# Two contraction tiles of both heads in each first weight piece, and products ordered by operand

## The chip, the cores and the metric

The kernel runs on one core of a Trainium2 chip. The metric is the device time of one execution in microseconds (us). Three runs of the kernel before gave 1209.47, 1212.88 and 1213.17 us; their median is 1212.88 us. A further, profiled execution took 1211.85 us.

## The reference

One decoder layer on a sequence of 1024 tokens with 1024 features, all in float32. RMSNorm, one input projection, 8 dilated attention heads beside 4 gated linear recurrences, an output projection with a residual, then a second RMSNorm and a gated MLP with a causal convolution. The change touches only the projection that makes the queries and keys of the first two attention heads:

```python
u = rms_norm(h, norm1_g[layer])
proj = u @ w_in[layer]
aq, ak, av, hq, hf, hi, hg = jnp.split(proj, IN_SPLITS, axis=-1)
attn = dilated_attention(aq.reshape(...), ak.reshape(...), av.reshape(...))
```

## The kernel before, in words

**Layout.** Features lie on the 128 partitions. The input is 8 contraction tiles `c` of 128 features by 1024 tokens; tokens are worked in two halves `hf` of 512. Each float32 operand is split into a high part and a low remainder, and a product is three TensorE matmuls: high weight by high input, high weight by low input, low weight by high input. The row scale of the RMSNorm (`R1`, and its transposed form `R1T`) is applied when a result leaves PSUM, so the products can start before the norm is known.

**Weight pieces.** `Ring` (L48) walks a plan of 256 KB pieces of 128x512. For each it starts a DMA from SyncE's queue into a raw buffer (L66; 5 raw buffers), makes the high part `whi` (L86, on ScalarE, but on VectorE for the very first piece) and the low part `wlo` (L88, on VectorE for keys in `on_vector`, else on GpSimd). Five pieces may be live; pieces in `aside` use other tiles (`thw`, `tlw`), which attention needs later. `done` gives a piece back and calls `fill`, which starts the next one of the plan.

**The first four pieces.** A head's query and key weights are 128 columns by 8 contraction tiles, 1024 numbers on each partition. The plan starts with head 0 tiles 0-3, head 1 tiles 0-3, head 0 tiles 4-7, head 1 tiles 4-7. Those of head 1 are the ones put aside. Then come four pieces of `V0` and four of `V1_0` for the attention values.

**Input.** `load_x` (L389) starts the DMA of one input tile, `scale_x` makes its high part `uhi` on ScalarE (L396) and its low part `ulo` on VectorE (L397). `square_x` and `sum_x` (L403, L408) build the sum of squares. The order of these and of the first four pieces is pinned on the queues by lines 421-445: x0, piece 0, x1, piece 1, x2, x3, pieces 2 and 3, x4 and on.

**Products.** TensorE runs in program order; the other engines are ordered by the scheduler of the framework, except where pinned. `dense` (L451) makes the products of one head and one half: for each `c` the matmuls of L459 (high, high), L461 (high, low input) and L462 (low weight). In the first half the order is head 0 tile 0, head 0 tile 1, head 1 tile 0, head 1 tile 1, and from tile 2 on head 0 and head 1 in turn (L665-670). `busy` (L378) puts matmuls of ones into an unused bank: eight at the start, and by `between` four after the first product, one after the third and two after the first product of tile 1. These make no result.

**Behind it.** The second half follows (L671). After its tile 2, `rms1(0)` makes R1 of the first half, both results of the first half leave PSUM (`evac`, L548-554) and `ring.fill()` starts the first `V0` pieces; pieces of the first heads are given back at tile 3 and tile 7 of the second half. Then come `V0` products (`tok`, L476-478), the scores of head 0 (`score_steps`, L584-596) and the long attention loop, in which the results of the second half leave PSUM. `tok`'s first two results and the scores share two PSUM banks, tag `s`.

Of the kernel before, what the change touches and what calls it, by code (L numbers as in the profile page):

```python
# [17 lines left out]
P = 128  # L18
SEQ = 1024
DM = 1024  # L20
NCT = DM // P
H2 = 512
# [21 lines left out]
def f32(ap):  # L44
    return ap.bitcast(F32)
# [93 lines left out]
class DownMix:  # L139
# [7 lines left out]
    def load(self, f, i, t):  # L147
        self.order(self.nc.sync.dma_start(t, self.w[2 * self.k + f, :, i * H2 : (i + 1) * H2]))
        return t
# [53 lines left out]
def hybrid_kernel(ctx: ExitStack, tc: tile.TileContext, xT, w_qk, w_tok, w_hg, w_out, w_up,  # L203
                  w_down, vecs, amask, hmask, out):
    nc = tc.nc
    PE, DVE, ACT, POOL = nc.tensor, nc.vector, nc.scalar, nc.gpsimd
# [12 lines left out]
    ones = f32(ones_r)  # L219
# [13 lines left out]
    halves = [slice(0, H2), slice(H2, SEQ)]  # L233


    plan = []
# [5 lines left out]
    def want_tok(key, g):  # L242
        for i in range(4):
            plan.append(((key, i), w_tok[g, i // 2, :, (i % 2) * H2 : (i % 2 + 1) * H2]))
# [14 lines left out]
    def want_hg(kind, h):  # L259
        want((kind, h), w_hg[4 * {"hq": 0, "hf": 1, "hg": 2}[kind] + h])  # L260

    for i in range(2):
        for h in range(2):
            plan.append(((("qk", h), i), w_qk[h, :, i * H2 : (i + 1) * H2]))
    want_tok("V0", 0)
    want_tok("V1_0", 1)
    for h in (2, 3, 4):
# [39 lines left out]
            xs = ("a11", "a12", "s1", "s2", "s3", "s4", "a22") if f == 2 else ("a11", "s1", "s2", "s3", "a12", "s4", "a22")  # L307
            plan += [((x, f), getattr(m, x)) for x in xs]
    ring = Ring(nc, ringp, plan)
    ring.on_vector = [("qk", 0), ("qk", 1), "V0"]  # L310

    def col(j):
        return vec[:, j : j + 1]
# [40 lines left out]
    uhi = up_.tile([P, NCT, SEQ], F32R, name="uhi")  # L354
    ulo = up_.tile([P, NCT, SEQ], F32R, name="ulo")
# [5 lines left out]
    def bank(tag, name):  # L361
        return ps1.tile([P, H2], F32, tag=tag, name=name, bufs=2)
# [7 lines left out]
    def aside(i):  # L370
        return tuple(at.tile([P, H2], F32R, tag=x, name=f"{x}w{i}", bufs=TB) for x in ("th", "tl"))

    ring.aside = {(("qk", 1), i): aside for i in range(2)}
    ring.aside["a12", 1] = None

    warm = bank("mm", "warm")

    def busy(n):  # L378
        for _ in range(n):
            PE.matmul(warm[:, :P], ones, ones, start=True, stop=True)  # L380

    busy(8)

    between = {(("qk", 0), 0, 0): (4, 1), (("qk", 0), 0, 1): (2, 0)}
    pin = tc.keep_in_program_order
    xts = {hf: vtile([P, NCT, H2], F32, f"xt{hf}") for hf in range(2)}

# [22 lines left out]
    def rms1(hf):  # L410
        ss = bank("t", f"ss{hf}")
        PE.matmul(ss, ones, sums[hf], start=True, stop=True)
        st = bank("t", f"sst{hf}")
        for i in range(4):
            PE.matmul(st[:, i : i + 1], sums[hf][:, i * P : (i + 1) * P], ones[:, 0:1], start=True, stop=True)
        rstd(R1[:, halves[hf]], rtile(f"ms{hf}"), rtile(f"rt{hf}"), ss, 1.0 / DM)
        tm = rv.tile([P, 64], F32, name=f"rst{hf}")
        rstd(R1T[:, 4 * hf : 4 * hf + 4], tm[:, 0:4], tm[:, 4:8], st[:, 0:4], 1.0 / DM)
# [32 lines left out]
    def dense(key, hf, evac, last, tag="mm"):  # L451

        t = halves[hf]
        ps = bank(tag, f"p{key}{hf}".translate({ord(x): "_" for x in "(', )"}))
        for c in range(NCT):
            hi, lo = ring.get((key, c // 4))
            s = slice((c % 4) * P, (c % 4 + 1) * P)
            b = between.get((key, hf, c), (0, 0))
            PE.matmul(ps, hi[:, s], uhi[:, c, t], start=(c == 0), stop=False)  # L459
            busy(b[0])  # L460
            PE.matmul(ps, hi[:, s], ulo[:, c, t], start=False, stop=False)  # L461
            PE.matmul(ps, lo[:, s], uhi[:, c, t], start=False, stop=(c == NCT - 1))  # L462
            busy(b[1])
            if last and c % 4 == 3:
                ring.done((key, c // 4))
            yield 0.65
        evac(ps)
# [60 lines left out]
    if True:  # L528
# [7 lines left out]
            kls.append(kl)  # L536
        qk = {}

        def qk_half(h, hf, last, tag="mm"):
            t = halves[hf]  # L540

            def evac(ps):
                if hf == 0:
                    qk[h] = (at.tile([P, SEQ], F32R, tag="qs", name=f"qs{h}", bufs=NQ),
                             at.tile([P, SEQ], F32R, tag="kh", name=f"kh{h}", bufs=NQ), kls[h % NQ])
                qs, kh, kl = qk[h]
                x = at.tile([P, H2], F32, tag="x", name=f"x{h}_{hf}")
                DVE.tensor_mul(x, ps, R1[:, t])  # L548
                ACT.mul(qs[0:64, t], x[0:64], DH ** -0.5)
                ACT.copy(kh[64:128, t], x[64:128])  # L550
                DVE.tensor_copy(kh[0:64, t], x[64:128])
                DVE.scalar_tensor_tensor(qs[64:128, t], x[0:64], DH ** -0.5, f32(qs[0:64, t]),
                                         op0=ALU.mult, op1=ALU.subtract)
                DVE.tensor_sub(kl[0:64, t], x[64:128], f32(kh[64:128, t]))
            return dense(("qk", h), hf, evac, last, tag)

        def qk_block(h):
            return [qk_half(h, 0, False), qk_half(h, 1, True)]
# [103 lines left out]
        lo4, hi4, all8 = range(4), range(4, 8), range(8)  # L662
        v0 = [tok("V0", t, v_evac(0), t == 7, "mm" if t > 1 else "s") for t in all8]

        pairs = [[qk_half(h, hf, hf == 1, "o" if hf else "mm") for h in range(2)] for hf in range(2)]  # L665
        for h in (0, 0, 1, 1):
            next(pairs[0][h])
        for c in range(2, NCT):
            for g in pairs[0]:
                next(g)  # L670
        for c in range(NCT):  # L671
            for g in pairs[1]:
                next(g)
            if c == 2:
                rms1(0)
                for g in pairs[0]:
                    next(g, None)
                ring.fill()
        for c in range(NCT):
            square_x(1, c)  # L680
# [29 lines left out]
        for h in range(NH):  # L710
            fill.add(*beside[h])
            for j in range(4):
                nxt = (h, j + 1) if j < 3 else (h + 1, 0)
                sc = score_steps(*nxt) if nxt[0] < NH else iter(())
                n_sc = 0 if nxt[0] == NH else (2 if nxt[1] < 2 else 4)
                va = value_steps(h, j, Ps)
                n_va = 2 * j + 2
                share = cost[h] / 4 / (n_sc + n_va)
                nPs = None
                k = 0  # L720
                if (h, j) == (NH - 1, 3):
                    fill.run(1.6)
                while True:
                    got = next(sc, None)
                    nPs = got or nPs
                    if got:
                        fill.run(share)
                    more = None
                    if not got or k % 2:
                        if h == 0 and k == 1 and j < 2:  # L730
                            next(pairs[1][j], None)
                        more = next(va, 0)
                        if more is None:
                            fill.run(share)
                    if not got and more == 0:
                        break
                    k += 1
                Ps = nPs
            fill.run()
# [16 lines left out]
    with pool("hg", "right") as hg:  # L756
# [13 lines left out]
        def f_half(h, hf, last):  # L770
            def evac(ps):
                nm = f"{h}_{hf}"
                A, B = ht("A", "A" + nm, 2), ht("B", "B" + nm, 2)
                DVE.tensor_mul(A, ps, R1[:, halves[hf]])
                DVE.tensor_scalar_max(A, A, -40.0)
                sigmoid(A, A)

                DVE.tensor_scalar(B, A, lb[:, 2 * NG + h : 2 * NG + h + 1], lb[:, NG + h : NG + h + 1],
                                  op0=ALU.mult, op1=ALU.add)
                ACT.activation(A, A, AF.Ln, bias=lb[:, h : h + 1], scale=lb[:, NG + h : NG + h + 1])  # L780
                gate[h, hf] = [A, B]
            return dense(("hf", h), hf, evac, last)

        def q_half(h, hf, last):
            def evac(ps):
                nm = f"{h}_{hf}"
                E, F = ht("E", "E" + nm, 2), ht("F", "F" + nm)
                DVE.tensor_mul(E, ps, R1[:, halves[hf]])
                DVE.tensor_scalar_max(F, E, -40.0)
                sigmoid(F, F)  # L790
                DVE.tensor_mul(E, E, F)
                gate[h, hf].append(E)
            return dense(("hq", h), hf, evac, last)
# [177 lines left out]
        for n, (h, hf) in enumerate(((0, 0), (0, 1), (1, 0), (1, 1), (2, 0), (3, 0), (2, 1), (3, 1))):  # L971

            at = 4.5 + 3 * n + 0.5 * (n in (0, 7))
            start = at - 1.1 if n == 7 else place["hq", h, hf]
# [264 lines left out]
    with pool("ps2", "left", space=PSUM) as ps2:  # L1239

        def bank2(name):
            return ps2.tile([P, H2], F32, tag="u", name=name, bufs=8)
# [69 lines left out]
        pairs = [(x, y, k) for x, y in STAGES for k in range(NPAIR)]  # L1312
# [86 lines left out]
        for x, y in STAGES:  # L1399
            last = x == "s4"  # L1400
# [9 lines left out]
            ps = [bank2(f"d{x}_{d}") for d in range(KS)]  # L1410
            for k in range(NPAIR):
                hi, lo = ring.get((("dn", x), k))
                ahi, alo = feed.get((y, k))
                for d in range(KS):
                    s = slice(d * P, (d + 1) * P)
# [102 lines left out]
```

## Time and profile before

| What | Value |
|---|---|
| median of three runs | 1212.88 us |
| the profiled execution | 1211.85 us |
| its span, first to last instruction | 1209.9 us |
| outside the span (difference of the two) | 1.95 us |
| mean granted TensorE clock | 0.996 |
| VectorE busy, share of the span | 79% |
| ScalarE busy, share of the span | 52% |
| GpSimd busy, share of the span | 25% |

A row of the timeline gives the start, the time until the end (of the whole group where it ends in xN with N over 1), engine, line, operation, written and read tiles, and in brackets how long the engine stood idle before and what released it. PE is TensorE, DVE VectorE, ACT ScalarE, POOL GpSimd and SPq the queue of SyncE. Matmuls are pipelined: the ends shown overlap the next starts, so a pace is read from the starts. A row of the windows gives the length of the stretch, then each engine's busy time, the granted TensorE clock (1.00 is full), the DMA share and GB/s.

### The profile page before, as it was taken

To read this page: it belongs to the slowest core of one execution; us is meant where nothing else is said; L and a number is where in the kernel's file an instruction comes from. 1 tells how busy PE (TensorE), PEld (TensorE's weight loads), DVE (VectorE), ACT (ScalarE), POOL (GpSimd) and SP (SyncE) were. 2 spreads that over 40 slices of the span, in tenths; PEclk is the share of its full clock that TensorE was granted. 3 is DMA by queue.
4 is the path that set the end of the run, shared out by engine and by line. 5 is a ranking of instruction groups with operands and counts; after the bars stand their busy time and mean duration, and the time that the engine had idled before them with its cause. 6 is when DMAs were issued, how large, how long until landed. Compare 5 with 4: busy or idle time off the path is not lost.

```text
span 1209.9 us, 17468 instructions
## 1 busy us (share of the span) xinstructions
PE 1193.9 (99%) x6014; PEld 1006.8 (83%) x6014; DVE 951.6 (79%) x1792; ACT 627.2 (52%) x1205; POOL 299.2 (25%) x278
## 2 busy tenths in 40 slices
PE   9999999999999999999999999999999999999996
PEld 7988888888888888888888888888888888888886
DVE  8867776666778776484999889898798878957986
ACT  8566667667656655454643343433434444444553
POOL 1254446545001014413221322312223100000000
PEclk9999999999999999999999999999999999999998
DMA  7021112123111123442023322333223267435532
GB/s 257 25 70 54 53 53 80 61 62 115 53 36 53 53 62 113 124 137 96 35 71 114 109 86 101 122 114 109 83 97 122 96 209 252 150 99 156 171 100 92
DMA packets 71817, 122.39 MB, mean 101 GB/s; under 512 B 7344, under 2 KB 17840, under 8 KB 71728
## 3 DMA queue, kind: packets, MB, share of 16 engines
q1 hardware_dynamic: 60928, 101.80, 26.8%
q10 hardware_dynamic: 10800, 19.47, 4.2%
q8 instruction: 47, 0.77, 0.3%
q14 instruction: 42, 0.34, 0.1%
HBM read 97.65 MB, written 23.59 MB: 100 GB/s over the span
## 4 chain that ended last, share of the span: by engine, by line
PE 93%; issue 2%; DVE 2%; ACT 1%; POOL 0%; DMA 0%; SPq 0%; DVEq 0%; ACTq 0%; POOLq 0%
PE p L1125 10%; PE p L1123 10%; PE p L1124 10%; PE ds L1418 3%; PE ds L1417 3%; PE ds L1416 3%; PE po L1027 2%; PE po L1029 2%; PE po L1028 2%; PE da L1418 2%; PE da L1417 2%; PE da L1416 2%; PE S L584 1%; PE piv L513 1%; PE S L585 1%
## 5 line engine op out<-in xcount | busy, mean ns | idle before, releaser
L88 POOL TENSOR_TENSOR wlo<-raww,whi 128x512 fp32r<-128x512 f32 x141 | 207.5, 1482 | 383.5 <-ACT whi L86 274.1
L86 ACT CAST whi<-raww 128x512 fp32r<-128x512 f32 x276 | 168.3, 618 | 190.6 <-DVE raww L120 64.8
L88 DVE TENSOR_TENSOR wlo<-raww,whi 128x512 fp32r<-128x512 f32 x136 | 97.4, 716 | 22.6 <-ACT whi L86 22.5
L86 ACT CAST whi<-r 128x512 fp32r<-128x512 f32 x70 | 43.6, 622 | 83.6 <-PE ds L1417 51.4
L596 POOL TENSOR_SCALAR P<-P,st 128x512 f32<-128x512 f32 (+2 forms) x96 | 56.3, 596 | 110.8 <-DVE st L593 62.2
L587 DVE CUSTOM_DVE_ANT_0 P<-S,mask 128x512 f32<-128x512 f32 (+2 forms) x96 | 52.1, 553 | 29.9 <-PE S L585 29.0
L592 ACT ACTIVATE P<-P,st 128x128 f32<-128x128 f32 (+3 forms) x64 | 49.7, 776 | 32.9 <-DVE st L587 16.6
L623 DVE TENSOR_TENSOR tl<-T,th 128x512 fp32r<-128x512 f32 (+1 forms) x80 | 50.7, 634 | 16.6 <-ACT th L622 15.6
L88 DVE TENSOR_TENSOR wlo<-r,whi 128x512 fp32r<-128x512 f32 x70 | 47.9, 686 | 20.2 <-ACT whi L86 20.1
L1418 PE MATMUL ds<-fhi,wlo 128*128 128x512 f32 x160 | 62.3, 389 | 0.0
L1417 PE MATMUL ds<-flo,whi 128*128 128x512 f32 x160 | 62.3, 389 | 0.0
L1416 PE MATMUL ds<-fhi,whi 128*128 128x512 f32 x160 | 62.2, 389 | 0.0
L1123 PE MATMUL p<-b1h,whi 128*128 128x512 f32 x160 | 62.2, 389 | 0.0
L1124 PE MATMUL p<-b1l,whi 128*128 128x512 f32 x160 | 62.2, 389 | 0.0
L1125 PE MATMUL p<-b1h,wlo 128*128 128x512 f32 x160 | 62.2, 389 | 0.0
L1145 DVE SCALAR_TENSOR_TENSOR cv<-g,vec,cv 128x511 f32<-128x511 f32 (+2 forms) x92 | 56.1, 615 | 4.7 <-ACT cv L1142 3.7
L1390 POOL TENSOR_TENSOR facc<-facc,sqf 128x256 f32<-128x256 f32 x4 | 2.9, 732 | 223.1 <-ACT sqf L1389 223.1
L1152 ACT ACTIVATE cv<-cv 128x512 f32<-128x512 f32 x44 | 27.8, 633 | 55.6 <-DVE cv L1145 55.5
L622 ACT CAST th<-T 128x512 fp32r<-128x512 f32 (+1 forms) x80 | 42.9, 536 | 23.5 <-PE T L615 20.9
L86 ACT CAST fhi<-rawf 128x512 fp32r<-128x512 f32 x70 | 43.1, 616 | 15.2 <-DMA rawf<-spT 6.5
L88 DVE TENSOR_TENSOR flo<-rawf,fhi 128x512 fp32r<-128x512 f32 x70 | 47.9, 684 | 4.0 <-ACT fhi L86 4.0
L1416 PE MATMUL da<-fhi,whi 128*128 128x512 f32 x120 | 46.7, 389 | 0.0
(670 smaller groups left out, 3833.5 us busy)
## 6 DMA issues: line engine op xcount, KB each, us to landing
raww<-in_w_up_dram SPq DMA_DIRECT2D x88, 256.0 KB, 3.1
raww<-in_w_tok_dram SPq DMA_DIRECT2D x52, 256.0 KB, 2.6
rawf<-spT SPq DMA_DIRECT2D x40, 256.0 KB, 2.7
r<-in_w_down_dram SPq DMA_DIRECT2D x40, 256.0 KB, 3.4
raww<-in_w_hg_dram SPq DMA_DIRECT2D x32, 256.0 KB, 2.6
raww<-in_w_out_dram SPq DMA_DIRECT2D x32, 256.0 KB, 2.6
spB<-a ACTq DMA_DIRECT2D x30, 256.0 KB, 2.3
spT<-t ACTq DMA_DIRECT2D x30, 256.0 KB, 2.0
```

What stands on the lines that cost most here:

```text
L86: self.pin(self.high(hi[:, :w], raw))
L88: self.pin(low.tensor_sub(lo[:, :w], raw, f32(hi[:, :w])))
L587: DVE.tensor_tensor_reduce(Pt[:, k0 : k0 + w], S[:, :w], mask[:, m : m + w], -1.0, BIG * 3, op0=ALU.add, op1=ALU.min, accum_out=st[:, k0 / ...
L596: POOL.tensor_scalar(e, e, st[:, 3:4], 1.0, op0=ALU.mult, op1=ALU.mult)
L623: DVE.tensor_sub(tl[:, :n], T[:, :n], f32(th[:, :n]))
L1123: PE.matmul(ps, hi[:, s], bhi, start=(start and n == 0), stop=False)
L1124: PE.matmul(ps, hi[:, s], blo, start=False, stop=False)
L1125: PE.matmul(ps, lo[:, s], bhi, start=False, stop=(stop and n == len(rhs) - 1))
L1145: DVE.scalar_tensor_tensor(dst, x, col(V_CW + j * NFF + f), dst, op0=ALU.mult, op1=ALU.add)
L1416: PE.matmul(ps[d], hi[:, s], ahi, start=(k == 0), stop=False)
L1417: PE.matmul(ps[d], hi[:, s], alo, start=False, stop=False)
L1418: PE.matmul(ps[d], lo[:, s], ahi, start=False, stop=(k == NPAIR - 1))
```

## The change

The four first pieces keep their size and count, but piece `i` now holds tiles 2i and 2i+1 of head 0 and of head 1, side by side. It is read with one DMA of two runs of 256 numbers (1 KB) per partition where before one run of 512 (2 KB) was read. Pieces 1 and 3 are the ones put aside. `first_two` takes the place of the two interleaved `dense` generators: for each tile it issues head 0 and head 1 with (high, high), then both with (high, low input), then both with (low weight, high input). The matmuls of ones between products go into a bank of tag `s`: two after the first pair, and one after each of the next three pairs, so five instead of seven. In the second half each piece is given back after its own pair of tiles, at tiles 1, 3, 5 and 7.

```diff
-    for i in range(2):
-        for h in range(2):
-            plan.append(((("qk", h), i), w_qk[h, :, i * H2 : (i + 1) * H2]))
+    def first_pair(i):
+        def load(ring):
+            t = ring.raw()
+            w = w_qk[0:2, :, 256 * i : 256 * (i + 1)]
+            ring.order(nc.sync.dma_start(t.rearrange("p (h n) -> p h n", h=2), w.rearrange("h p n -> p h n")))
+            return t
+        return load
+    for i in range(4):
+        plan.append((("qk01", i), first_pair(i)))
...
-    ring.on_vector = [("qk", 0), ("qk", 1), "V0"]
+    ring.on_vector = ["qk01", "V0"]
...
-    ring.aside = {(("qk", 1), i): aside for i in range(2)}
+    ring.aside = {("qk01", i): aside for i in (1, 3)}
...
-    between = {(("qk", 0), 0, 0): (4, 1), (("qk", 0), 0, 1): (2, 0)}
...
+        def first_two(hf, tag):
+            t = halves[hf]
+            ps = [bank(tag, f"p01_{hf}_{h}") for h in range(2)]
+            idle = bank("s", "idle") if hf == 0 else None
+            waits = {(0, 0): 2, (0, 1): 1, (0, 2): 1, (1, 0): 1} if hf == 0 else {}
+            for c in range(NCT):
+                hi, lo = ring.get(("qk01", c // 2))
+                for i, (w, u) in enumerate(((hi, uhi), (hi, ulo), (lo, uhi))):
+                    for h in range(2):
+                        s = slice(256 * h + (c % 2) * P, 256 * h + (c % 2 + 1) * P)
+                        PE.matmul(ps[h], w[:, s], u[:, c, t], start=(c == 0 and i == 0), stop=(c == NCT - 1 and i == 2))
+                    for _ in range(waits.get((c, i), 0)):
+                        PE.matmul(idle[:, :P], ones, ones, start=True, stop=True)
+                if hf and c % 2:
+                    ring.done(("qk01", c // 2))
+                yield
+            for h in range(2):
+                qk_evac(h, hf)(ps[h])
+                yield
...
-        pairs = [[qk_half(h, hf, hf == 1, "o" if hf else "mm") for h in range(2)] for hf in range(2)]
-        for h in (0, 0, 1, 1):
-            next(pairs[0][h])
-        for c in range(2, NCT):
-            for g in pairs[0]:
-                next(g)
+        pairs = [first_two(hf, "o" if hf else "mm") for hf in range(2)]
         for c in range(NCT):
-            for g in pairs[1]:
-                next(g)
+            next(pairs[0])
+        for c in range(NCT):
+            next(pairs[1])
             if c == 2:
                 rms1(0)
-                for g in pairs[0]:
-                    next(g, None)
+                for _ in pairs[0]:
+                    pass
                 ring.fill()
```

More of the change, by code (lines that the diff above doesn't have):

```diff
@@ L371, in aside @@
         return tuple(at.tile([P, H2], F32R, tag=x, name=f"{x}w{i}", bufs=TB) for x in ("th", "tl"))
-    ring.aside = {(("qk", 1), i): aside for i in range(2)}
+    ring.aside = {("qk01", i): aside for i in (1, 3)}
     ring.aside["a12", 1] = None
     warm = bank("mm", "warm")
[L378 to L382, printed above, removed]
-    between = {(("qk", 0), 0, 0): (4, 1), (("qk", 0), 0, 1): (2, 0)}
+    for _ in range(8):
+        PE.matmul(warm[:, :P], ones, ones, start=True, stop=True)
     pin = tc.keep_in_program_order
@@ L457, in dense @@
             s = slice((c % 4) * P, (c % 4 + 1) * P)
-            b = between.get((key, hf, c), (0, 0))
             PE.matmul(ps, hi[:, s], uhi[:, c, t], start=(c == 0), stop=False)
-            busy(b[0])
             PE.matmul(ps, hi[:, s], ulo[:, c, t], start=False, stop=False)
             PE.matmul(ps, lo[:, s], uhi[:, c, t], start=False, stop=(c == NCT - 1))
-            busy(b[1])
             if last and c % 4 == 3:
@@ L537, in hybrid_kernel, with qk_evac @@
         qk = {}
+        def first_two(hf, tag):
[17 more added lines that the diff above has]
+                yield
         def qk_half(h, hf, last, tag="mm"):
+            return dense(("qk", h), hf, qk_evac(h, hf), last, tag)
+        def qk_evac(h, hf):
             t = halves[hf]
@@ L554, in evac @@
                 DVE.tensor_sub(kl[0:64, t], x[64:128], f32(kh[64:128, t]))
-            return dense(("qk", h), hf, evac, last, tag)
+            return evac
         def qk_block(h):
@@ L730, in hybrid_kernel @@
                         if h == 0 and k == 1 and j < 2:
-                            next(pairs[1][j], None)
+                            next(pairs[1])
                         more = next(va, 0)
```

## The prediction

> **What bounds the kernel now.** I read the page first, for its span and the busy time of the engines.
>
> ```profile
> span 1209.9 us, 17468 instructions
> PE 1193.9 (99%) x6014; PEld 1006.8 (83%) x6014; DVE 951.6 (79%) x1792; ACT 627.2 (52%) x1205; POOL 299.2 (25%) x278
> ```
>
> TensorE is busy for 1193.9 of 1209.9 us, so at most 16 us of the span are without a matmul. Then I asked the waits of TensorE over the whole span; its columns are microseconds in total, times, and the longest.
>
> ```profile
> PE T L612 <- POOL P L596: 2.6, 1, 2.6
> PE warm L380 <- DVE ones L229: 1.1, 1, 1.1
> PE p__qk___0_0_211 L459 <- DVE whi L86: 0.8, 1, 0.8
> PE S L584 <- DVE st L587: 0.8, 2, 0.4
> PE p L1125 <- POOL wlo L88: 0.5, 1, 0.5
> PE ssf L1365 <- POOL facc L1390: 0.3, 1, 0.3
> ```
>
> The waits sum to 6.1 us. Only 0.8 us of them lie where the change works, at the first real product, and they end with the first weight piece's high part. The largest, 2.6 us, lies some 50 us behind it. The windows show what that one costs:
>
> ```profile
> 58.00:61.00 3.00, 1.95 (x12) 1.43 (x10) 2.97 (x7) 1.51 (x4) 1.95 (x2) 1.00 0.00 0
> 61.00:64.00 3.00, 1.34 (x8) 1.24 (x9) 1.58 (x7) 2.31 (x6) 2.08 (x3) 0.90 0.24 87
> 64.00:67.00 3.00, 3.00 (x14) 2.71 (x13) 1.76 (x5) 1.07 (x2) 1.86 (x4) 0.53 0.25 87
> ```
>
> In the third stretch TensorE is busy throughout, but at a granted clock of 0.53. Lost clock is 0.10 x 3 + 0.47 x 3 = 1.7 us. So this stall is worth 2.6 + 1.7 = 4.3 us, far more than anything in the start. It will carry two rivals.
>
> The timeline of the first microseconds shows the place of the change.
>
> ```profile
> 4.38 1.13 DVE L86 CAST whi<-raww 128x512 fp32r<-128x512 f32 x1 [3.25 <-DMA raww<-in_w_qk_dram]
> 5.66 0.47 PE L459 MATMUL p__qk___0_0_211<-uhi,whi 128*128 128x512 f32 x1 [0.83 <-DVE whi L86]
> 5.97 1.05 PE L380 MATMUL warm<-ones 128*128 128x128 f32 x8
> 6.16 1.53 DVE L397 SCALAR_TENSOR_TENSOR ulo<-xt,vec,uhi 128x512 fp32r<-128x512 f32 x2
> 6.18 0.72 ACT L396 ACTIVATE uhi<-xt,vec 128x512 fp32r<-128x512 f32 x1 [1.65 <-DMA xt<-in_xT_dram]
> 6.96 0.50 PE L461 MATMUL p__qk___0_0_211<-ulo,whi 128*128 128x512 f32 x1
> 7.53 0.38 PE L380 MATMUL warm<-ones 128*128 128x128 f32 x2
> 7.98 0.61 PE L380 MATMUL warm<-ones 128*128 128x128 f32 x4
> 8.24 0.69 DVE L88 TENSOR_TENSOR tlw<-raww,thw 128x512 fp32r<-128x512 f32 x1 [0.55 <-ACT thw L86]
> 8.90 0.39 PE L459 MATMUL p__qk___1_0_225<-uhi,thw 128*128 128x512 f32 x1
> 10.29 0.39 PE L459 MATMUL p__qk___0_0_211<-uhi,whi 128*128 128x512 f32 x1
> ```
>
> The last row is head 0's first product of tile 2. From 8.90 to 10.29 lie the six products of head 1's first two tiles, so one product takes 1.39 / 6 = 0.23 us. A filler matmul of ones leaves two records: eight records in 1.05 us make four fillers of 0.26 us. From 6.96 to 10.29 TensorE issues eleven products and three fillers (the six records at 7.53 and 7.98): 11 x 0.23 + 3 x 0.26 = 3.31 of 3.33 us. So from 6.96 us on TensorE never waits in the kernel before. The second weight piece, split at 8.24 + 0.69 = 8.93 us, does not hold it up, though the order by heads looks as if it would. The only slack that the change can use lies ahead of 6.96 us, and the end of that is set by the low part of the first input tile, not by weights: two VectorE operations run 6.16 to 7.69, so the first is done at about 6.92.
>
> **The change part by part.**
>
> *The products.* Before 6.96 us the kernel before issues one product (head 0) and four fillers. The changed one issues two products and two fillers: 5.66 + 2 x 0.23 + 2 x 0.26 = 6.64 us, then it waits 0.3 us for that low part. The two dropped fillers therefore bring nothing; they covered a wait. From 6.96 us on the changed kernel needs ten products and three fillers to reach tile 2: 10 x 0.23 + 3 x 0.26 = 3.08, so 10.04 where the old one takes 3.31 by the same prices. The gain is one product, 0.23 us. Everything else that `first_two` does is the same number of products in another order.
>
> *The pieces.* Each row of a piece is now read as two runs of 1 KB. No such load stands in the busy start of the trace. The nearest rows are the later value pieces, which have just this shape (line 252), against loads with runs of 2 KB (line 66 between 30 and 120 us). First stands the landing of line 252, then that of line 66; then the queue's row for the stretch of 30 to 120 us (2 KB) and for 200 to 250 us (mostly 1 KB).
>
> ```profile
> DMA to landing us min/median/max: 2.4/2.6/3.3
> DMA to landing us min/median/max: 2.3/2.6/3.0
> q1 hardware_dynamic: 2433, 4.43, 15.6%
> q1 hardware_dynamic: 4481, 4.56, 29.9%
> ```
>
> The medians say that 1 KB runs cost nothing; the least differ by +0.1 and the greatest by +0.3. Below nothing I go as far as the least differ, to -0.1. The queue's rows say otherwise: 0.156 x 16 engines x 90 us / 2433 = 92 ns for a packet of mostly 2 KB, and 0.299 x 16 x 50 / 4481 = 53 ns for one of mostly 1 KB. A piece is 8 packets of 2 KB per engine, 0.74 us, or 16 of 1 KB, 0.85 us. I take 0.11 us, since the start is a stretch where the queue works without a pause and time per packet is what counts there. The Trainium skill, "DMA: Bandwidth & Descriptors", section Specifications, names 512 B as the least transfer for line rate; by that rule the halved runs would cost nothing and the whole 0.23 us would remain. The packet rows speak against the rule, the medians for it.
>
> With piece 0 later by 0.11 us the chain behind it shifts as a whole: the cast, the low parts behind it on VectorE, and the product at 6.96. It may shift less. So this part costs +0.11 us, with bounds -0.1 and +0.3.
>
> Four pieces lie ahead of input tile 4 on the queue, so tile 4 lands up to 4 x 0.11 = 0.44 us later. What hides this is the lead of the low part:
>
> ```profile
> 11.53 0.75 DVE L397 SCALAR_TENSOR_TENSOR ulo<-xt,vec,uhi 128x512 fp32r<-128x512 f32 x1
> 13.25 0.39 PE L461 MATMUL p__qk___0_0_211<-ulo,whi 128*128 128x512 f32 x1
> ```
>
> It is done at 12.28 and used at 13.25: 0.97 us of lead. In the new order the low part is used after two products of the tile instead of one, so by starting 0.23 us sooner the tile needs it at the same time. The cover holds at 0.44. At the upper bound, 4 x 0.3 = 1.2 us, it would be overdrawn by 0.2 us. The second piece has more room: it is first needed at tile 2, about 10.04 us, where before it was needed at 8.90.
>
> *The giving back.* In the second half, piece 0 is given back after tile 1, so `fill` starts all four `V0` pieces ahead of `rms1(0)` in program order, where before three came behind it and the fourth after tile 3. The first `V1_0` piece follows tile 5, not tile 7: nine products or 2.1 us earlier. These are the same loads, casts and subtractions, on SyncE's queue, ScalarE, VectorE and GpSimd, in another order. The rows that say who could wait for them:
>
> ```profile
> 18.20:30.00 11.80, 11.80 (x55) 9.53 (x54) 11.80 (x23) 11.54 (x24) 0.00 (x0) 1.00 0.43 154
> 29.34 0.68 DVE L88 TENSOR_TENSOR wlo<-raww,whi 128x512 fp32r<-128x512 f32 x1
> 31.15 0.28 PE L476 MATMUL pV<-whi,uhi 128*128 128x256 f32 x1
> 31.90 1.29 POOL L88 TENSOR_TENSOR wlo<-raww,whi 128x512 fp32r<-128x512 f32 x1 [26.67 <-ACT whi L86]
> 31.95 1.80 DVE L408 TENSOR_TENSOR sq<-sq,sq 128x512 f32<-128x512 f32 x1
> 38.47 0.48 DVE L567 SCALAR_TENSOR_TENSOR v<-pV,R1T,v 128x256 fp32r<-128x256 f32 x1
> 39.95 0.33 PE L584 MATMUL S<-kh,qs 128*128 128x256 f32 x1
> 42.61 0.17 DVE L593 RECIPROCAL st<-st 128x1 f32<-128x1 f32 x1 [0.59 <-ACT P L592]
> ```
>
> VectorE works without a gap from 18.2 to 30 us, and the row at 42.61, where it waits for ScalarE, is the first of the timeline behind that with an idle mark. Up to there a changed order moves its work about, but not the end of its sum. The last `V0` split ends at 30.02, ahead of the first product at 31.15 that uses the piece group. A VectorE addition took 1.80 us beside the GpSimd split that began at 31.90, so 1.1 us more than the 0.69 of such an operation: that hold now falls some 2 us earlier, on the norm's chain. TensorE's nearest user is the second score matmul at 39.95, which needs the bank that the value result leaves at 38.47 + 0.48 = 38.95: 1.0 us of lead. I put this part at nothing, with bounds of -4.3 and +4.3 us, worked out with the rivals.
>
> The sum: -0.23 + 0.11 = -0.1 us (bounds -0.33 and +0.3 for the start, the overdraft of 0.2 included). On the profiled execution that is 1211.85 - 0.1 = 1211.7 us. The median of the runs shown stands 1.0 us above that execution, and the runs themselves lie 3.7 us apart.
>
> **The rivals.**
>
> *The stall at 60 us goes (faster).* A product of the loop waits there for GpSimd's normalising, which waits for VectorE:
>
> ```profile
> 59.12 1.28 POOL L88 TENSOR_TENSOR wlo<-raww,whi 128x512 fp32r<-128x512 f32 x1 [0.45 <-ACT whi L86]
> 59.29 1.13 DVE L591 TENSOR_TENSOR st<-st 128x1 f32<-128x1 f32 x1
> ```
>
> A 128x1 operation took 1.13 us while GpSimd split a `V1_0` piece. If the new ring order let that split slip behind, over 1 us of the wait would go, and with a shorter gap perhaps the clock loss too; at best all of it: 1211.7 - 4.3 = 1207.4 us. For it speaks that the scheduler orders these engines anew. Against it: this split belongs to the second `V1_0` piece, released by the last `V0` products, which the change does not touch, and the pair at 42.61 shows that VectorE's backlog does not reach across from the start.
>
> *A new stall at the scores (slower).* If over 1.0 us of other VectorE work is put ahead of the value result at 38.47, the score matmul at 39.95 waits. From 1.0 us on each further microsecond is lost one for one. With 3.6 us put ahead, the gap is 2.6 us, as long as the one at 60 us, and if it takes the clock too it costs 4.3: 1211.7 + 4.3 = 1216.0 us. For it: four splits now precede the norm's chain in the program, and GpSimd's hold falls on that chain. Against it: this is work that lay ahead of 38.47 before as well. The clock's part rests on the row of 0.53. The Trainium skill, "TensorE: Matmul & The Clock Gate", section Part 1, has the clock fall after an idle window of about 3.4 us; by that rule a gap of 2.6 us would cost itself alone and the case would end at 1214.3. The row disagrees: 2.6 us of waiting was enough here.
>
> *The pieces eat the gain (not what the change says).* At the upper end, +0.3 for landing and the overdraft, the start ends 0.3 us slower, 1212.1 us. That can't be told from the forecast by the time, only by the profile.
>
> **How the numbers follow.** About 0.3% (3.6 us) is what a measurement of this kernel can tell from no change. The forecast and the third rival are both within it, 0.87 together, 0.70 and 0.17. The vanished stall gets 0.07 and the new stall 0.06: both need a reordering that reaches TensorE, and only those two pass 0.3%. The likeliest case's own range is the bounds of the start, 1211.5 to 1212.1, widened to the spread of the runs of the kernel before, 1209.5 to 1213.2. Part of the two outer cases (a stall of 1 to 2 us more or less) is to be held too, so I take 1208.5 to 1214.3 us.
>
> **What would show it.** Right: two products ahead of 6.96 us, a wait of about 0.3 us behind them, the first product of tile 2 near 10.15 us where it was 10.29, no wait of TensorE until the one at 60 us, and that one still near 2.6 us with a clock near half behind it. Wrong: a wait at tile 2 or 4 for weights or input, a product at 6.96 that comes over 0.3 us later, a wait at the scores near 40 us, or another length of the stall at 60 us. A time off by more than 3.6 us with that stall unchanged would overthrow the argument.

## The result, and the profile after

The changed kernel took 1218.59 us (median of 6 runs, 1218.08 to 1219.43). The kernel before took 1211.67 us beside it (6 runs, 1209.47 to 1213.17). The ratio is 1.0058, with a 95% interval from 1.0048 to 1.0068. So the change cost 6.9 us where I had forecast 0.1 us less, and the time lies above the range that I gave. The profiled execution took 1218.23 us. Every ratio below is to the kernel before, run beside the kernel in question.

The page's first lines of the kernel after: the span is 6.4 us longer, while TensorE's busy time grew by 1.3 us only. So most of the loss is waiting.

```profile
span 1216.3 us, 17460 instructions
PE 1195.2 (98%) x6010; PEld 1006.9 (83%) x6010; DVE 945.2 (78%) x1792; ACT 630.8 (52%) x1205; POOL 299.4 (25%) x278
```

The waits of TensorE after (total, times, longest):

```profile
PE p L1144 <- DVE a L1175: 4.9, 1, 4.9
PE T L637 <- POOL P L621: 2.6, 1, 2.6
PE S L609 <- DVE v L592: 1.2, 2, 0.8
PE warm L386 <- DVE ones L229: 1.1, 1, 1.1
PE S L609 <- DVE st L612: 0.9, 3, 0.4
PE ssf L1386 <- POOL facc L1411: 0.3, 1, 0.3
PE p L551 <- DVE whi L86: 0.2, 1, 0.2
PE p L551 <- DVE ulo L399: 0.2, 1, 0.2
```

Two rows have no counterpart before: 1.2 us at the scores (L609) and 4.9 us at a product `p` of the MLP (L1144). The second stands some 560 us behind the last edited instruction. The old 2.6 us stall is unchanged.

The timeline of the start, after:

```profile
4.33 0.43 DVE L86 CAST whi<-raww 128x512 fp32r<-128x512 f32 x1 [3.20 <-DMA raww<-in_w_qk_dram]
4.87 0.95 POOL L534 MEMSET kl<- 64x1024 f32 x1
6.20 0.74 PE L551 MATMUL p<-ulo,whi 128*128 128x512 f32 x2 [0.15 <-DVE ulo L399]
9.29 0.62 PE L551 MATMUL p<-uhi,thw 128*128 128x512 f32 x2
```

The cast takes 0.43 instead of 1.13 us, and tile 2 starts at 9.29 instead of 10.29: the start itself gained a whole microsecond in this profile. The place of the long wait, after:

```profile
605.10 0.39 PE L1146 MATMUL p<-b1h,wlo 128*128 128x512 f32 x1
609.66 0.68 DVE L1175 TENSOR_TENSOR a<-p1v,cv 128x512 f32<-128x512 f32 x1
610.39 0.80 PE L1144 MATMUL p<-b1h,whi 128*128 128x512 f32 x1 [4.90 <-DVE a L1175]
610.98 0.63 PE L1145 MATMUL p<-b1l,whi 128*128 128x512 f32 x1
611.41 0.63 PE L1146 MATMUL p<-b1h,wlo 128*128 128x512 f32 x1
```

The row at 605.10 is the twelfth and last matmul of the main loop's first product. The second product, at 610.39, waits until VectorE has read `p1v`, the last result of the plain blocks that open the MLP. In the kernel before, VectorE read that result no sooner, and the second product did not wait for it:

```profile
605.59 0.39 PE L1123 MATMUL p<-b1h,whi 128*128 128x512 f32 x1
609.91 0.68 DVE L1154 TENSOR_TENSOR a<-p1v,cv 128x512 f32<-128x512 f32 x1
```

Neither reads the other's data; what they can share is the PSUM bank, which the experiments below test. The matmuls behind the gap start 0.43 us apart where the pace is 0.23. The windows after show the clock:

```profile
605.00:611.00 6.00, 1.10 (x5) 0.58 (x4) 6.00 (x13) 1.38 (x4) 0.00 (x0) 0.80 0.37 119
611.00:616.00 5.00, 5.00 (x14) 3.97 (x13) 5.00 (x9) 2.82 (x5) 0.00 (x0) 0.56 0.18 67
```

Twelve matmuls at 0.43 instead of 0.23 us are 2.3 to 2.4 us, so this one wait costs 4.9 + 2.3 = 7.2 us.

How far TensorE is ahead or behind, by the start of the same instruction in the two profiled executions:

| Instruction | before, us | after, us | difference |
|---|---|---|---|
| first product of tile 2 | 10.29 | 9.29 | -1.00 |
| first `V0` product | 31.15 | 30.73 | -0.42 |
| second score matmul | 39.95 | 41.18 | +1.23 |
| transpose behind the stall at 62 us | 62.66 | 63.95 | +1.29 |
| first product of the MLP's main loop | 602.87 | 602.60 | -0.27 |
| end of the span | 1209.9 | 1216.3 | +6.4 |

The step from +1.29 to -0.27 comes from the clock behind the 2.6 us stall. In the profile of the kernel before it fell (a loss of 1.7 us); in this one it did not:

```profile
60.00:64.00 4.00, 1.29 (x9) 0.91 (x8) 3.86 (x12) 1.86 (x5) 2.08 (x3) 1.00 0.19 66
64.00:68.00 4.00, 4.00 (x31) 3.83 (x32) 2.23 (x8) 3.42 (x7) 3.27 (x5) 1.00 0.25 66
```

From -0.27 the wait at the MLP adds 7.2 us, and a wait of 0.5 us for a weight split (L1125 in the kernel before) no longer occurs: -0.27 + 7.2 - 0.5 = 6.4 us, as measured.

**Why a bank.** The kernel takes its PSUM tiles from a pool, and tiles with the same tag take turns in that tag's two banks. A tag gets them when it is first used, as the placement below shows. Before, the tags were first used in the order mm, o, t, s. The changed kernel asks for the bank of the fillers, `bank("s", "idle")`, ahead of all but mm, so the order is mm, s, o, t. The MLP's main loop has a pool of its own on the same eight banks, and takes them in the same order in both kernels. The placement in the two programs as built:

```
tile                                   bank before   bank after
fillers between the first products          0             2
tag o                                     2, 3          4, 5
tag t                                     4, 5          6, 7
tag s                                     6, 7          3, 2
last result of the plain blocks (t)         5             7
main loop, products 1 to 7            0, 7, 6, 1, 5, 4, 2 (both)
```

Before, the second product asks for bank 7, which a tag `s` result left long ago, and the last result lies in bank 5, asked for by the fifth product. After, the last result lies in bank 7, asked for by the second. From about 45 us on, the order of the instructions on VectorE, ScalarE, GpSimd and SyncE is the same in both kernels.

### The profile page after: what moved, and what is told of

The parts are those of the page before. It is cut to its first block, busy times and chain, and to the rows that moved or that the text cites. A ratio compares the mean times of both kernels' runs of the same rounds, so it can differ in the third digit from the quotient of the medians.

```text
span 1216.3 us, 17460 instructions
## 1 busy us (share of the span) xinstructions
PE 1195.2 (98%) x6010; PEld 1006.9 (83%) x6010; DVE 945.2 (78%) x1792; ACT 630.8 (52%) x1205; POOL 299.4 (25%) x278
## 4 chain that ended last, share of the span: by engine, by line
PE 89%; DVE 7%; ACT 2%; issue 1%; DMA 1%; SPq 0%; POOL 0%; DVEq 0%; ACTq 0%; POOLq 0%
PE p L1144 10%; PE p L1145 10%; PE p L1146 10%; PE ds L1438 3%; PE ds L1437 3%; PE ds L1439 3%; PE po L1048 2%; PE po L1050 2%; PE po L1049 2%; PE da L1438 2%; PE da L1437 2%; PE da L1439 2%; PE S L609 1%; PE piv L512 1%; PE piv L514 1%; PE piv L513 1%
## 5 line engine op out<-in xcount | busy, mean ns | idle before, releaser
L1144 PE MATMUL p<-b1h,whi 128*128 128x512 f32 x160 | 63.4, 396 | 4.9 <-DVE a L1175 4.9
L1438 PE MATMUL da<-flo,whi 128*128 128x512 f32 x120 | 46.7, 389 | 0.0
```

The costliest lines, as they stand in the source:

```text
L1144: PE.matmul(ps, hi[:, s], bhi, start=(start and n == 0), stop=False)
L1438: PE.matmul(ps[d], hi[:, s], alo, start=False, stop=False)
```

## The experiments

Theory A: the 4.9 us wait is the bank, and the bank comes from the fillers' tag alone. Theory B: VectorE comes late to the MLP because its order at the start was changed.

**One word undone.** The changed kernel with the fillers (the matmuls of ones) in a tag that would be used second anyway.

```diff
-            idle = bank("s", "idle") if hf == 0 else None
+            idle = bank("o", "idle") if hf == 0 else None
```

> The changed kernel with one word altered: the matmuls of ones between the first products go into a bank of tag o instead of tag s. The tags then take their PSUM banks in the order mm, o, t, s again, as in the kernel before; every other queue's order is the one of the changed kernel. Theory A (banks): the 4.9 us wait at 605 us is the second product of the MLP's main loop meeting the bank that the last result of the plain blocks still holds, and this comes from the tags' order alone. Then the wait and the half clock behind it (12 products at 0.43 instead of 0.23 us, 2.3 us) go: about 1218.6 - 7.2 = 1211.4 us. Theory B (order): VectorE reaches the MLP late because its work at the start was reordered; then the wait stays and the time is about 1218.6 us.

Measured: 1212.21 us, ratio 1.0007 (0.9998 to 1.0016). Its two longest waits of TensorE:

```profile
PE T L637 <- POOL P L621: 2.6, 1, 2.6
PE S L609 <- DVE v L592: 1.2, 2, 0.7
```

The row of L1144 is gone and 6.4 us with it; the score wait stays. Theory B falls: the orders of the other engines are those of the changed kernel, and VectorE read the last result at 609.66 us in the changed kernel against 609.91 before, so it was not late.

**One word done.** The kernel before, with its fillers in a bank of tag s.

```diff
-            busy(b[0])
+            busy(b[0], idle)
...
+        idle = bank("s", "idle") if (key, hf) == (("qk", 0), 0) else None
```

> The kernel before with its seven fillers between the first products put into a bank of tag s instead of the unused bank of tag mm; all orders on the engines and the pieces are those of the kernel before. Theory A (banks): the same wait of about 4.9 us and the half clock behind it appear near 605 us, about 1211.7 + 7.2 = 1218.9 us. Theory B (order): no change, 1211.7 us.

Measured: 1218.54 us, ratio 1.0060 (1.0048 to 1.0073). Waits of TensorE:

```profile
PE p L1124 <- DVE a L1155: 4.8, 1, 4.8
PE T L613 <- POOL P L597: 2.6, 1, 2.6
```

The old pieces, the old order of products, and yet the whole loss. Seven matmuls whose result nobody reads cost 0.6% by the tag that they were given.

**The same bank freed from the other end.** The fillers stay in tag s; in the plain blocks the tags o and t are exchanged, so the last two results lie in banks 4 and 5.

```diff
-    q0 = {"g": bank("s", "p1g"), "v": bank("o", "p1v")}
+    q0 = {"g": bank("s", "p1g"), "v": bank("t", "p1v")}
...
-    p1 = {("g", 0): p1, ("g", 1): bank("o", "p1g1")}
+    p1 = {("g", 0): p1, ("g", 1): bank("t", "p1g1")}
...
-        p1["v", hf] = bank("t", f"p1v{hf}")
+        p1["v", hf] = bank("o", f"p1v{hf}")
```

> The changed kernel with its fillers left in tag s, and in the plain blocks at the start of the MLP the tags o and t exchanged: the last two results lie in the banks of o (4 and 5) and the two before them in those of t (6 and 7). The orders on VectorE, ScalarE, GpSimd and SyncE are those of the changed kernel. Theory A (banks): what counts is only which bank the last result holds when the second product of the main loop asks for bank 7, so the 4.9 us wait and the half clock go here too: about 1218.6 - 7.2 = 1211.4 us, as with the fillers in tag o. Rival (something else that the fillers' bank brings, at the start or in the scores): the wait stays, about 1218.6 us.

Measured: 1213.43 us, ratio 1.0019 (1.0010 to 1.0028). The wait is gone here too, though the time is 2.0 us above the 1211.4 expected and some 1.2 us above that with the fillers in o. Of these 1.2 us, 0.7 are waits for weight splits in the MLP that the other did not have (0.7 and 0.5 here, 0.5 there); the rest stays open:

```profile
PE p L1146 <- POOL wlo L88: 0.7, 1, 0.7
PE p L1146 <- DVE wlo L88: 0.5, 1, 0.5
```

**The giving back.** Fillers in o, and the first pieces given back where the kernel before did.

```diff
-                if hf and c % 2:
-                    ring.done(("qk01", c // 2))
+                if hf and c % 4 == 3:
+                    ring.done(("qk01", c // 2 - 1))
+                    ring.done(("qk01", c // 2))
```

> As the kernel with the fillers in tag o, and the first pieces given back where the kernel before did, two at tile 3 and two at tile 7 of the second half. VectorE and ScalarE then have the order of the kernel before. Theory A with the giving back: the 1.2 us wait of the score matmuls near 40 us comes from the four splits that passed the norm, so it goes: about 1211.4 - 1.2 = 1210.2 us, and what is left of the start's gain (tile 2 at 9.3 instead of 10.3 us) shows at the end. Rival: the score wait comes from TensorE being earlier than VectorE can follow; then it stays and the time is that of the kernel with the fillers in o, 1211.4 us.

Measured: 1210.80 us, ratio 0.9999 (0.9990 to 1.0008), 1.4 us below the kernel with the early giving back, which ran beside it eleven times as well (the means lie 1.5 us apart, with a standard error of 0.4). Waits of TensorE:

```profile
PE T L638 <- POOL P L622: 2.6, 1, 2.6
PE warm L386 <- DVE ones L229: 1.1, 1, 1.1
PE S L610 <- DVE st L613: 0.8, 2, 0.4
```

The score wait for the value result (`v`) is gone. So it was the early return: in the kernel after, VectorE's low part of the second value result starts at 40.65 us, behind all seven of the squares' additions, where the kernel before had it at 38.47, behind four.

```profile
40.05 0.68 DVE L410 TENSOR_TENSOR sq<-sq,sq 128x512 f32<-128x512 f32 x1
40.65 0.48 DVE L592 SCALAR_TENSOR_TENSOR v<-pV,R1T,v 128x256 fp32r<-128x256 f32 x1
```

**The cast.** The kernel before, with the two memsets of kl moved to where no cast can meet them. A second profile of the kernel before goes with it.

```diff
     TB = 3
+    NQ = 2
+    kls = []
+    for i in range(NQ):
+        kl = at.tile([P, SEQ], F32R, name=f"kl{i}")
+        POOL.memset(f32(kl[64:128]), 0.0)
+        kls.append(kl)
...
-        NQ = 2
-        kls = []
-        for i in range(NQ):
-            kl = at.tile([P, SEQ], F32R, name=f"kl{i}")
-            POOL.memset(f32(kl[64:128]), 0.0)
-            kls.append(kl)
```

> The kernel before with the two GpSimd memsets of kl moved ahead of its scaling of the vector table, so that none runs while VectorE casts the first weight piece. Theory C (the start's gain is the cast, which took 1.13 us beside a memset and 0.43 us without): the first product starts near 5.0 instead of 5.66 us, tile 2 near 9.6 instead of 10.3 us, about 1211.0 us. Rival (the start's gain is the new order of products and pieces): the cast stays near 1.1 us, tile 2 at 10.3 us, 1211.7 us.

> The kernel before once more, for a second look at its start. If the cast of the first weight piece meets the memset only in some executions, it takes 0.43 us here and tile 2 starts near 9.5 us; if it is a property of the kernel before, 1.1 us and 10.3 us. The time is that of the kernel before, 1209.5 to 1213.2 us.

Measured: 1211.09 us with the memsets moved, ratio 1.0000 (0.9991 to 1.0009). The cast took 0.43 us and tile 2 started at 9.55:

```profile
9.55 0.39 PE L465 MATMUL p__qk___0_0_211<-uhi,whi 128*128 128x512 f32 x1
```

The kernel before, profiled again, took 1211.14 us. Its cast took 0.48 us without any edit, and tile 2 started at 9.73:

```profile
4.27 0.48 DVE L86 CAST whi<-raww 128x512 fp32r<-128x512 f32 x1 [3.14 <-DMA raww<-in_w_qk_dram]
9.73 0.40 PE L459 MATMUL p__qk___0_0_211<-uhi,whi 128*128 128x512 f32 x1
```

So the 1.13 us was one execution's, not the kernel's. The cast starts about when GpSimd's second memset becomes due. First the memset of the first profile, which began 0.09 us ahead of the cast, then that of the second profile, which began during the cast:

```profile
4.29 0.95 POOL L535 MEMSET kl<- 64x1024 f32 x1
4.54 1.11 POOL L535 MEMSET kl<- 64x1024 f32 x1
```

So it looks as if whichever begins first holds the other up; the memset was first in this one profile only. Moving the memsets gains nothing that shows in the time.

**The changed kernel again.**

> The changed kernel once more, for a second look. The wait at 605 us and the score wait near 40 us stay, 4.9 and 1.2 us. If the clock behind the stall at 62 us depends on the moment, it may be below 1.00 here where it was full in the first profile. The time is 1218.1 to 1219.4 us.

Measured: 1217.74 us. The 4.8 us wait stays, the score wait is 1.1 us (0.6 of it put down to ScalarE's half of the value result), and the clock behind the 2.6 us stall is full again:

```profile
60.00:64.00 4.00, 1.36 (x12) 1.13 (x11) 3.16 (x9) 2.25 (x4) 2.48 (x4) 1.00 0.20 66
64.00:68.00 4.00, 4.00 (x33) 3.82 (x32) 2.61 (x8) 3.43 (x7) 3.28 (x4) 1.00 0.19 66
```

**The stall at 62 us.** My first rival priced it; here it is tried. The kernel with the fillers in o and the late giving back, and three low parts of `V1_0` on VectorE:

```diff
+        ring.on_vector += ["V1_0"]
```

> The kernel with the fillers in tag o and the late giving back, and three more low parts (second to fourth piece of V1_0) on VectorE instead of GpSimd. Theory D (the 2.6 us stall near 62 us is VectorE held for 1.1 us by a GpSimd split, then the normalising behind it): the stall shrinks by about 0.9 us, and the clock loss of up to 1.7 us behind it may go: 1210.8 - 0.9 = 1209.9 down to 1208.2 us. Rival (VectorE is the bound there and gets three more operations of 0.69 us): the stall stays or grows, 1210.8 to 1212.9 us.

Measured: 1208.35 us, ratio 0.9983 (0.9974 to 0.9992): 0.17% below the kernel before. The stall is 0.9 us shorter, and the 128x1 operation that the GpSimd split had held for 1.13 us takes 0.15. The wait of TensorE, then VectorE's timeline:

```profile
PE T L638 <- POOL P L622: 1.7, 1, 1.7
```

```profile
58.91 0.15 DVE L617 TENSOR_TENSOR st<-st 128x1 f32<-128x1 f32 x1
```

In this profile the clock still fell behind the shorter stall, by 0.30 x 4 + 0.13 x 4 = 1.7 us:

```profile
60.00:64.00 4.00, 2.64 (x12) 2.45 (x13) 3.37 (x10) 2.31 (x6) 1.14 (x2) 0.70 0.39 115
64.00:68.00 4.00, 4.00 (x30) 3.86 (x30) 2.98 (x8) 1.61 (x3) 2.65 (x3) 0.87 0.06 20
```

**The same in the kernel before.**

> The kernel before with the same three low parts of V1_0 on VectorE, nothing of the change in it. If the gain of the kernel with these splits on VectorE is the shorter stall alone (1.7 instead of 2.6 us), this one has it too: a stall of 1.7 us near 61 us and a ratio to the kernel before of about 0.998 to 0.999, 1208.4 to 1209.9 us. If the changed start has a part in it beyond its 0.2 us, this one stays at 1.000, 1210.9 us.

Measured: 1209.03 us, ratio 0.9979 (0.9971 to 0.9988), with the stall at 1.7 us and, in its profile, no loss of clock:

```profile
60.00:64.00 4.00, 2.65 (x19) 2.48 (x20) 3.74 (x13) 2.68 (x7) 1.15 (x2) 1.00 0.34 108
64.00:68.00 4.00, 4.00 (x37) 4.00 (x36) 2.72 (x8) 3.51 (x8) 3.85 (x5) 1.00 0.25 89
```

The gain is the same without the change, so none of it is the change's. The shorter stall is 0.9 us of it. The rest is more than one profile can account for; that the clock falls in fewer executions would fit, since seven of the twelve executions of the kernel with the fillers in o and these splits took 1208.1 to 1208.4 us, and the profiled one, which lost clock, 1210.29 us, but no profile of the faster ones shows it.

## Why the prediction was wrong, point by point

**The step that failed** is the sentence "Everything else that `first_two` does is the same number of products in another order." It priced the fillers by their number and passed over their bank. The changed `idle = bank("s", "idle")` is the first use of a tag, and with it the tags o, t and s change their banks for the rest of the pool's life. That is worth the whole loss: 7.6 us when it alone is added to the kernel before (1218.54 against 1210.98 us beside it), 6.4 us when it alone is taken from the changed one (1218.59 to 1212.21). No rival had this mechanism. The only place past the start that I looked at was the stall at 62 us; the product at 602 us had no wait in the trace before, so nothing in a row pointed there. What would have pointed there is in the code: a pool whose tags are placed by first use, and a second pool on the same banks.

**One product, 0.23 us: right at its place, unseen in the time.** From the first product with a low input to tile 2 the kernel after takes 3.09 us (6.20 to 9.29) and the kernel before 3.33 us (6.96 to 10.29); I had worked out 3.08 and 3.31. The start of tile 2 alone does not show it: it lay at 9.29 to 9.90 us in the six profiles with the new order and at 9.55 to 10.29 us in the five with the old, because the cast (0.43 to 1.13 us) and the pace of the first products (0.27 us each in the first profile of the kernel after, 0.50 with the fillers in o) differ from one execution to the next. With the bank and the early return undone the ratio is 0.9999, so the gain cannot be told from none there.

**The two dropped fillers bring nothing: right.** The low part of the first input tile ends a wait ahead of the second pair, as forecast, but for 0.15 us instead of 0.3, and sooner than 6.96 us because the cast was shorter.

**The pieces, +0.11 us: 0.05 in the mean, not settled.** The first cast, which waits for the first piece, began between 4.29 and 4.36 us in six profiles with 1 KB runs (mean 4.32) and between 4.22 and 4.38 in five with 2 KB runs (mean 4.27): 0.05 us later in the mean, with ranges that overlap, so 0.11 is neither borne out nor excluded. What was mis-sized more is the base: tile 2 at 10.29 us was the slow end of a start that lay at 9.73 in the second profile of the same kernel. The wait at tile 4 that I had named as a sign of being wrong did come in the first profile of the kernel after: the tile, started at 12.02 us, would have used its low part two products later, at 12.48, and that part was done at 12.67.

```profile
11.92 0.75 DVE L399 SCALAR_TENSOR_TENSOR ulo<-xt,vec,uhi 128x512 fp32r<-128x512 f32 x1
12.72 0.73 PE L551 MATMUL p<-ulo,whi 128*128 128x512 f32 x2
```

It cost 0.24 us there. The other five profiles with the new order do not have it (in its second profile the low part was done at 11.97 us and used at 12.50).

**The giving back, nothing: wrong, a term put too low.** The rival of a new stall at the scores had the place and the cause (splits ahead of the norm push the value results back) and gave it 0.06. It happened in every profile with the early return, at 1.1 to 1.2 us. My reason against it, that all this work lay ahead of 38.47 us before as well, does not hold: three of the squares' additions lay behind it, and passed the value results when the norm's chain came later (its last operation starts at 31.96 us in the kernel after and at 28.67 before, behind all four splits instead of among them).

**The stall at 62 us: right as a mechanism.** Its length did not change, and freeing VectorE from GpSimd's hold shortened it by 0.9 us. The Trainium skill, "GPSIMD Engine Reference", section 1. Specifications, says that GpSimd shares its SBUF interface with VectorE and contends with those of its operations that have two SBUF inputs or run in a 2-port mode. The 128x1 operation has two inputs, and its rows of 1.13 against 0.15 us agree. The cast has one, and no row here shows its mode; it took 1.13 against 0.43 us.

**The sum.** Going by the ratios, the word costs 0.51% (1.0058 against 1.0007 with the fillers in o) and the early return 0.08% (1.0007 against 0.9999). What is left is 0.9999 (0.9990 to 1.0008), so the part that I worked out, -0.1 us, is not contradicted. It is not shown either: a tenth of a microsecond is far inside that interval. The first profiles of the two kernels also differ by the 1.7 us of clock behind the 62 us stall. Both profiles of the kernel after kept that clock; whether most of its executions do is not shown.

## What to carry to other kernels

A scratch tile is not free because nobody reads it: its allocation takes part in how a pool lays out its banks, and where a later pool lies on the same banks, one tag used sooner can make an early writer wait for a late reader. When an edit adds, drops or moves the first use of a tag, compare where every later tile lies and who asks for each bank next, before looking at a single duration. And take the start of a kernel from more than one profile: whether VectorE's cast or GpSimd's memset began first made 0.6 us of difference between two executions of the same program.

## What the runs showed of the hardware

The length of a short gap does not decide what it costs in clock. A gap of 2.6 us near 62 us stands in nine profiles: in seven it was followed by a loss of 1.7 us of clock, in the two of the kernel after by none. A gap of 1.7 us cost 1.7 us in one kernel (fillers in o, three splits on VectorE) and nothing in another (the kernel before with these splits). The place in the span does not decide it either: the gaps without a loss ended at 63.24 and 63.95 us, and others that ended at 63.43 (tags exchanged) and 63.74 us (fillers in o) had one. Where the clock is lost, the loss is the same, half clock for about 3.4 us, as in the kernel before:

```profile
63.00:63.50 0.50, 0.50 (x6) 0.50 (x5) 0.00 (x0) 0.50 (x1) 0.50 (x2) 0.92 0.00 0
63.50:66.50 3.00, 3.00 (x12) 2.61 (x11) 1.36 (x4) 1.55 (x4) 1.86 (x3) 0.50 0.25 87
66.50:67.00 0.50, 0.50 (x5) 0.50 (x4) 0.40 (x1) 0.00 (x0) 0.50 (x2) 0.67 0.00 0
```

The Trainium skill, "TensorE: Matmul & The Clock Gate", section Part 1, describes a free-running window of 3.4 us; a loss of all or nothing that lasts 3.4 us agrees with that. What its phase was in an execution no profile here shows. Its rule that the clock falls after an idle window of about 3.4 us does not agree: 1.7 us was enough.
